# Adding to the residual by accumulating DMAs in the MLP stages of a hybrid decoder trunk

## The chip, the cores and the metric

The kernel runs on one core of one Trainium2 chip. The metric is device time in microseconds (us) of one execution. Three runs of the kernel before took 1236.65, 1238.46 and 1238.83 us; their median is 1238.46.

The core has five engines with a queue each, which run side by side and wait for each other by semaphores: TensorE (PE, the matmuls; PEld is its weight load), VectorE (DVE), ScalarE (ACT), GpSimd (POOL) and SyncE (SP, which here only starts transfers). Each engine works its own queue in order. Transfers (DMAs) are started from the queues of SP, ACT and POOL and are carried out by 16 DMA engines. Matmuls write to PSUM, from where DVE or ACT take the results; POOL works on the other on-chip memory, SBUF.

## What is computed

Two layers of a decoder trunk on x of 512 positions by 1024 features, in float32. Each layer first adds a mixing block (attention, short convolution and a recurrent part in parallel, then an output projection), then an MLP. What the change touches is the last two lines:

```python
for l in range(DEPTH):
    h = rms_norm(x, norm_mix_g[l])
    ...
    x = x + mixed @ w_out[l]
    h = rms_norm(x, norm_mlp_g[l])
    x = x + jnp.square(jax.nn.relu(h @ w_mlp_up[l])) @ w_mlp_down[l]
return rms_norm(x, final_norm_g)
```

The MLP is 1024 wide outside and 4096 inside.

## The kernel before

**Layout.** x is held transposed in SBUF, as eight tiles x[0] to x[7] of 128 features by 512 positions. A weight block is 128 by 128. To keep float32 accuracy, every weight and every operand is split into a rounded part and a remainder (`whi`/`wlo`, `mh`/`ml`, `shi`/`slo` and so on), and one product is three matmuls: hi x hi, hi x lo, lo x hi. The rounded part is made by ACT (a cast), the remainder by DVE or POOL (a subtraction). So each weight block costs a load, an ACT cast and a DVE subtraction before PE can use it.

**The mixing part** of each layer is ordered by hand. The MLP part, which the change touches, is written as a plain program, and the Tile framework orders each engine's queue from that program with its own estimate of times. Instructions of neighbouring groups are therefore interleaved. It also inserts every semaphore wait, and a buffer ring (`bufs=2` and so on) makes a new tile wait until the last user of its slot is done.

**The MLP of a layer.**
- `up(i)`, four plain up groups, and after that `two(i0, i1)`, fourteen paired up groups. `two` computes two up groups together from 2 x 2 blocks with seven half-width products in place of eight (Strassen's scheme in Winograd's form): sums of weight blocks (`s1` to `s4`) times sums of activation blocks (`th`, made once by `blocks`). Its products go to the PSUM tiles `pa`, `pb` and `pc`; ACT copies partial results out of PSUM (L1522, L1530, L1534, L1545), DVE adds them (L1541, L1546, L1549). The sums `s1` and `s3` of the next pair are made by DMA in `summed`: SP loads one weight half (L1475), then POOL's queue adds the other by an accumulating DMA (L1476).
- Each up result is squared and split by `square` and `kept` into `mh` and `ml` (POOL makes most `ml`, L1409). Four such tiles form the operand of one down step h.
- `down(h, js)` adds to x[j] what four middle tiles contribute. h runs from 0 to 7 (to 5 in the second layer, whose rest is `last_group`), and each h is done in two halves of four outputs j. A half is issued after each `two`, and the halves that are left come one behind the other at the end.
- A half of `down` is either **direct** or a **quad**. Direct (L1674 to L1679): for each j, twelve matmuls of 512 columns into one PSUM tile (`dn`), then one addition on DVE, `x[j] = pt + x[j]` (L1677). Quad (`quad`, for the pairs named in `DN_QUADS`: h = 2, 4, 6 in the first layer, h = 2, 4 in the second, both halves each): two pairs of outputs (j, j+1) with the same seven-product scheme at 256 columns. Its PSUM tiles are `qa`, `qb`, `qc`. `turn_blocks` prepares the activation sums for it.

**In a quad**, for each of its two j: r0 and r1 are raw weights (`rawq`, ring `raw` of three buffers, L1610), from which DVE makes the sums `s2q` and `s4q` (L1614 to L1618). ACT copies products out as `p1q`, `p5q`, `u2q`, `c1q` (L1599). DVE builds c0 in two halves: the left (L1634) and the right (L1644). c0 is the whole first output of the pair, 128 x 512, and is added to x[j] by DVE (`add`, L1595, seen in the trace as `x<-c0q`). The second output is added to x[j+1] in two halves of 256 columns (`x<-c1q` and `x<-qa`), also at L1595. c0 has a ring of two buffers (tag `c0`), which it shares with the c0 of `two` (L1541) and with `turn_blocks`. The ring with the tag `sq` has two buffers of 128 x 512 and serves the norms.

The loads of the raw weights all go through SP's queue, which waits in order for free buffers. POOL's queue holds in the MLP the `ml` remainders and the accumulating DMAs of `summed`.

Of the kernel before, what the change touches and what calls it, by code (L numbers as in the profile page):

```python
# [10 lines left out]
F32 = mybir.dt.float32  # L11
# [5 lines left out]
ALU = mybir.AluOpType  # L17
# [5 lines left out]
S = 512  # L23
P = 128
# [161 lines left out]
WHOLE = 5  # L186
PT = 1
N_TWO = (NG_UP - N_ONE) // 2
MID = tuple(range(N_ONE)) + tuple(N_ONE + i + N_TWO * j for i in range(N_TWO) for j in range(2))


# [82 lines left out]
def tile_trunk(ctx: ExitStack, tc: tile.TileContext, xT, wts, prm_d, cst_d, lora_d, gup_d, lam_d, fin_d, hd_d, out):  # L274
    nc = tc.nc
    act, dve, pool = nc.scalar, nc.vector, nc.gpsimd
# [23 lines left out]
    wp = Pool(ctx.enter_context(tc.tile_pool(name="wp", bufs=2)), "wp")  # L300
# [3 lines left out]
    def psum(tag, bufs, name):  # L304
        return ps.tile([P, 512], F32, tag=tag, bufs=bufs, name=name)
# [3 lines left out]
    x = [cp.tile([P, S], F32, tag=f"x{j}", name=f"x{j}") for j in range(NK)]  # L309
# [23 lines left out]
    def weights(g, k0=0, k1=NK, home=None):  # L333

        for a in range(k0, k1, 4):
            n = min(4, k1 - a)
            turn[0] += 1
            if home is None and spare[0] and turn[0] % (WB + 1) == 0:
                pool_, tags, bufs = spare[0], ("raw4", "whi4", "wlo4"), 1
            else:  # L340
                pool_, tags, bufs = wp, ("raw", "whi", "wlo"), WB
            raw = pool_.tile([P, 4, P], F32, tag=tags[0], bufs=bufs, name=f"raw{g}_{a}")
            nc.sync.dma_start(raw[:, :n].rearrange("p k c -> p (k c)"), wts[g, :, a * P:(a + n) * P])
            if home is None:
                hi, lo = [pool_.tile([P, 4, P], F32R, tag=t, bufs=bufs, name=f"w{p}{g}_{a}") for p, t in zip(("hi", "lo"), tags[1:])]
            else:
                hi, lo = home(a)
            act.copy(hi[:, :n], raw[:, :n])  # L348
            (pool if a and lean[0] else dve).tensor_tensor(lo[:, :n], raw[:, :n], hi[:, :n].bitcast(F32), ALU.subtract)  # L349
            for k in range(n):  # L350
                yield hi[:, k], lo[:, k]
# [9 lines left out]
    def mm3(out_ps, w, acts, n=NK):  # L361
        for _ in mm3_steps(out_ps, w, acts, n):
            pass
# [12 lines left out]
    def norm_tile(j, key):  # L376

        if j == 0:
            acc = wp.tile([P, S], F32, tag="acc", bufs=1, name=f"acc{key}")
            nrm[key] = [acc]  # L380
            act.activation(acc, x[j], AF.Square)
        else:
            sq = wp.tile([P, S], F32, tag="sq", bufs=2, name=f"sq{key}_{j}")
            act.activation(sq, x[j], AF.Square)
            dve.tensor_tensor(nrm[key][0], nrm[key][0], sq, ALU.add)
# [182 lines left out]
    for l in range(L):  # L568
# [826 lines left out]
        with ExitStack() as mx:  # L1395
# [73 lines left out]
            def summed(p, name):  # L1469

                if p < N_TWO:
                    i0, i1 = N_ONE + p, N_ONE + N_TWO + p
                    t = sums[p, name] = fp.tile([P, 4, P], F32, tag=name, bufs=2, name=f"{name}{l}_{i0}")
# [99 lines left out]
            def quad(h, half):  # L1573
# [9 lines left out]
                def product(pt, w, ks, moving, first, last):  # L1583
                    for i, k in enumerate(ks):
                        ahi, alo = moving(i)
                        whi, wlo = [t[:, k] for t in w]
                        pe.matmul(pt, whi, ahi, start=first and i == 0, stop=False, skip_group_check=True)
                        pe.matmul(pt, whi, alo, start=False, stop=False, skip_group_check=True)
                        pe.matmul(pt, wlo, ahi, start=False, stop=last and i == 1, skip_group_check=True)
# [4 lines left out]
                def add(j, q, pt):  # L1594
                    dve.tensor_tensor(x[j][:, q], pt, x[j][:, q], ALU.add)  # L1595

                def copied(name, pt, n):
                    t = fp.tile([P, H], F32, tag=name, bufs=2, name=f"{name}q{n}")
                    act.copy(t, pt)  # L1599
                    return t  # L1600
# [4 lines left out]
                for i in range(2):  # L1605
                    j = 4 * half + 2 * i
# [17 lines left out]
                for step in ((0, 1), (2, 3), (5, 4), (6,)):  # L1624
                    for j, w0, s12, s34, w22, (pa, pb, pc) in ab:
                        n = f"{l}_{h}_{j}"
                        for c in step:
                            if c == 0:
                                product(pa, w0, (0, 2), blk(0, 0), True, False)
                                keep["p1", j] = copied("p1", pa, n)  # L1630
                            elif c == 1:
                                product(pc, w0, (1, 3), blk(1, 0), True, True)
                                keep["c0", j] = c0 = fp.tile([P, S], F32, tag="c0", bufs=2, name=f"c0q{n}")
                                dve.tensor_tensor(c0[:, left], pc, keep["p1", j], ALU.add)  # L1634
                            elif c == 2:
                                product(pb, s12, (0, 1), trn(0), True, False)
                                keep["p5", j] = copied("p5", pb, n)
                            elif c == 3:
                                product(pa, s12, (2, 3), trn(1), False, False)
                                keep["u2", j] = copied("u2", pa, n)  # L1640
                            elif c == 5:
                                product(pb, s34, (2, 3), blk(1, 1), False, True)
                                c0 = keep["c0", j]
                                dve.tensor_tensor(c0[:, right], pb, keep["u2", j], ALU.add)  # L1644
                                add(j, slice(0, S), c0)
                            elif c == 4:
                                product(pa, s34, (0, 1), trn(2), False, False)
                                c1 = copied("c1", pa, n)
                                dve.tensor_tensor(c1, c1, keep["p5", j], ALU.add)
                                add(j + 1, right, c1)  # L1650
                            else:
                                product(pa, w22, (0, 1), trn(3), False, True)
                                add(j + 1, left, pa)

            def down(h, js):

                if (h, js[0] // 4) in DN_QUADS[l]:
                    quad(h, js[0] // 4)
                    return
                g, k0 = h // 2, 4 * (h % 2)  # L1660
                if h == 0 and js[0] == 0:
                    pts = [psum(("at", "mm")[j], 2, f"dn{l}_{h}_{j}") for j in js[:2]]
                    ws = [list(weights(wbase + NG_IN + NG_OUT + NG_UP + 8 * g + j, k0, k0 + 4)) for j in js[:2]]
                    for a, b in ((0, 3), (3, 4)):
                        for j, pt, w in zip(js, pts, ws):
                            for k in range(a, b):
                                (whi, wlo), (ahi, alo) = w[k], mids[k]
                                pe.matmul(pt, whi, ahi, start=(k == 0), stop=False)
                                pe.matmul(pt, whi, alo, start=False, stop=False)
                                pe.matmul(pt, wlo, ahi, start=False, stop=(k == 3))  # L1670
                    for j, pt in zip(js, pts):
                        dve.tensor_tensor(x[j], pt, x[j], ALU.add)
                    js = js[2:]
                for j in js:  # L1674
                    pt = psum(*(("mm", 2), ("rp", 4))[j % 2], f"dn{l}_{h}_{j}")
                    mm3(pt, weights(wbase + NG_IN + NG_OUT + NG_UP + 8 * g + j, k0, k0 + 4), mids[4 * h:4 * h + 4], 4)
                    dve.tensor_tensor(x[j], pt, x[j], ALU.add)  # L1677
                    if h == 2 * N_KG - 1 and j < NK - LATE:
                        norm_tile(j, f"m{l + 1}")  # L1679

# [8 lines left out]
            h, half = 0, 1  # L1689
            for p in range(N_TWO):  # L1690
                ms = two(N_ONE + p, N_ONE + N_TWO + p)
                if len(mids) >= 4 * h + 6 and h < 2 * N_KG - 2 * (l == L - 1):
                    down(h, range(4 * half, 4 * half + 4))
                    h, half = h + half, 1 - half
# [3 lines left out]
            while h < 2 * N_KG - 2 * (l == L - 1):  # L1698
                down(h, range(4 * half, 4 * half + 4))
                h, half = h + half, 1 - half  # L1700
# [11 lines left out]
def _layout(inputs):  # L1712
# [7 lines left out]
    for l in range(L):  # L1720
# [7 lines left out]
        for g in range(4):  # L1728
            w[b + 8 * g:b + 8 * g + 8] = groups(a["w_mlp_down"][l].reshape(NG_UP, P, D)[list(MID[8 * g:8 * g + 8])].reshape(D, D))
    prm = np.zeros((L, P, N_PRM), np.float32)  # L1730
# [41 lines left out]
```

## Time and profile before

| | |
|---|---|
| profiled execution | 1238.0 us, of which the span from first to last instruction is 1236.2 us |
| granted TensorE clock | 0.997 of full |
| accumulating DMAs from POOL's queue | 52, of 256 KB each |
| plain loads of weights from SP's queue | 323 (`raw`) and 40 (`rawq`) of 256 KB |
| DVE additions to x in the MLP | 68 direct (L1677), 20 `x<-c0q`, 20 `x<-c1q`, 20 `x<-qa` |
| matmuls | 10090 |

In the timeline views a row gives the start in us from the span's start, the length in us, the engine, the source line, the operation and its tiles (`out<-in`); a note in brackets gives the idle time of that engine just before the row and what ended it. Rows of one engine may overlap a little, since an instruction can start while the one before it still writes. A wait row gives who waited for whom, the us in total, how often, and the longest. PE's ends are modelled, so short idle times of PE read a little smaller than they are.

### The profile page before, as it was taken

The page shows a single profiled execution, that of the slowest core. Times are in us where ns is not written, and L with a number is a line of the kernel's source. Part 1 is how long each engine was busy: PE and PEld are TensorE (multiplying, and loading weights), DVE is VectorE, ACT ScalarE, POOL GpSimd, SP SyncE. Part 2 cuts the span into 40 slices and gives each one's busy share as a digit, 9 for nine tenths or more (in the row PEclk, how much of TensorE's full clock was granted, in tenths as well). Part 3 has the DMA queues.
Part 4 walks back from the last instruction along what each step waited for, and adds up shares of the span by engine and source line. Part 5 has one row for each costly group of instructions (what it writes and reads, how often), then busy time and mean ns, then how long its engine had stood idle before and what let it go on. Part 6 is the DMA issues. An engine that isn't in the chain of part 4 may idle for free. (4 is left out here: it accounts for less than half of the span.)

```text
span 1236.2 us, 26900 instructions
## 1 busy us (share of the span) xinstructions
PE 1217.8 (99%) x10090; PEld 1065.6 (86%) x10090; DVE 1011.3 (82%) x2023; ACT 742.6 (60%) x1606; POOL 386.0 (31%) x502
## 2 busy tenths in 40 slices
PE   9999999999999999999999999999999999999997
PEld 7788788888999989889888888888889898998987
DVE  7787888879888998989867777787897999899654
ACT  7785755557456655656675656564775566565543
POOL 2264636331122121121126354553302212222111
PEclk9999999999999999999999999999999999999998
DMA  6523333125653463631235243322456645446122
GB/s 225 159 90 108 111 86 102 53 96 169 190 146 108 128 180 98 168 86 52 94 113 159 82 133 118 94 70 69 145 172 147 152 110 158 128 118 177 54 78 77
DMA packets 95506, 148.48 MB, mean 120 GB/s; under 512 B 22544, under 2 KB 26384, under 8 KB 95376
## 3 DMA queue, kind: packets, MB, share of 16 engines
q1 hardware_dynamic: 87168, 132.39, 34.5%
q0 software_dynamic: 7488, 13.63, 7.2%
q8 instruction: 79, 1.29, 0.5%
q10 hardware_dynamic: 720, 0.75, 0.2%
q14 instruction: 51, 0.42, 0.1%
HBM read 137.56 MB, written 9.18 MB: 119 GB/s over the span
## 5 line engine op out<-in xcount | busy, mean ns | idle before, releaser
L694 POOL TENSOR_TENSOR wlo<-raw,whi 128x512 fp32r<-128x512 f32 x84 | 112.1, 1336 | 203.8 <-ACT whi L682 167.3
L287 PE MATMUL pj<-ahim,whi 128*128 128x512 f32 x392 | 156.7, 400 | 0.0
L287 PE MATMUL pj<-ahim,wlo 128*128 128x512 f32 x392 | 156.5, 399 | 0.0
L287 PE MATMUL pj<-alom,whi 128*128 128x512 f32 x392 | 156.0, 398 | 0.0
L1476 POOL DMA_DIRECT2D s<-wts x52 | 48.0, 922 | 293.3 <-DVE slo_p L1491 68.5
L1409 POOL TENSOR_TENSOR ml<-m,mh 128x512 fp32r<-128x512 f32 x56 | 82.3, 1518 | 178.9 <-ACT mh L1408 63.1
L682 ACT CAST whi<-raw 128x512 fp32r<-128x512 f32 x142 | 87.6, 618 | 70.3 <-PE pj L287 26.5
L287 PE MATMUL dn<-mh,whi 128*128 128x512 f32 x288 | 112.3, 390 | 0.0
L287 PE MATMUL dn<-ml,whi 128*128 128x512 f32 x288 | 112.2, 390 | 0.0
L287 PE MATMUL dn<-mh,wlo 128*128 128x512 f32 x288 | 112.1, 390 | 0.0
L1490 ACT CAST shi_p<-s 128x512 fp32r<-128x512 f32 x112 | 70.0, 625 | 65.1 <-PE pa L287 35.1
L287 PE MATMUL pa<-thi,shi_p 128*128 128x256 f32 x336 | 95.6, 285 | 4.5 <-ACT c L1545 3.9
L287 PE MATMUL pa<-tlo,shi_p 128*128 128x256 f32 x336 | 94.8, 282 | 0.0
L287 PE MATMUL pa<-thi,slo_p 128*128 128x256 f32 x336 | 94.4, 281 | 0.0
L1491 DVE TENSOR_TENSOR slo_p<-s,shi_p 128x512 fp32r<-128x512 f32 x112 | 76.5, 694 | 17.8 <-ACT shi_p L1490 16.6
L348 ACT CAST whi<-raw 128x512 fp32r<-128x512 f32 x86 | 52.9, 620 | 56.2 <-PE dn L287 30.7
L287 PEld LDWEIGHTS pj<-alom,whi 128*128 128x128 f32 x392 | 73.9, 188 | 14.0 <-issue 0.5
L287 PEld LDWEIGHTS pj<-ahim,wlo 128*128 128x128 f32 x392 | 73.9, 188 | 13.8 <-issue 0.2
L287 PEld LDWEIGHTS pj<-ahim,whi 128*128 128x128 f32 x392 | 73.8, 188 | 13.7 <-issue 0.3
L349 DVE TENSOR_TENSOR wlo<-raw,whi 128x512 fp32r<-128x512 f32 x86 | 72.5, 846 | 10.7 <-ACT whi L348 10.7
L1490 ACT CAST shi_p<-raw 128x512 fp32r<-128x512 f32 x84 | 52.4, 624 | 33.6 <-PE pb L287 18.1
L287 PEld LDWEIGHTS pa<-thi,shi_p 128*128 128x128 f32 x336 | 63.0, 188 | 6.1 <-ACT c L1545 4.7
(649 smaller groups left out, 3905.2 us busy)
## 6 DMA issues: line engine op xcount, KB each, us to landing
raw<-wts SPq DMA_DIRECT2D x323, 256.0 KB, 2.8
s<-wts SPq DMA_DIRECT2D x52, 256.0 KB, 3.6
s<-wts POOLq DMA_DIRECT2D x52, 256.0 KB, 4.4
rawq<-wts SPq DMA_DIRECT2D x40, 256.0 KB, 2.9
qs<-dqhi SPq DMA_DIRECT2D x24, 128.0 KB, 3.4
ks<-dkhi SPq DMA_DIRECT2D x24, 128.0 KB, 3.6
x<-xT SPq DMA_DIRECT2D x8, 256.0 KB, 4.8
dqhi<-qhi SPq DMA_DIRECT2D x6, 256.0 KB, 3.2
```

The lines of the kernel that those rows point to most:

```text
L287: ins = nc.tensor.matmul(*a, **k)
L348: act.copy(hi[:, :n], raw[:, :n])
L349: (pool if a and lean[0] else dve).tensor_tensor(lo[:, :n], raw[:, :n], hi[:, :n].bitcast(F32), ALU.subtract)
L682: yield act.copy(hi[:, k0:k1], raw[:, k0:k1])
L694: yield eng.tensor_tensor(lo[:, k0:k1], raw[:, k0:k1], hi[:, k0:k1].bitcast(F32), ALU.subtract)
L1409: (dve if i < 4 else pool).tensor_tensor(lo, m, hi.bitcast(F32), ALU.subtract)
L1476: pool.dma_start(t.rearrange("p k c -> p (k c)"), of[1], accum_op=ALU.add)
L1490: act.copy(hi, src)
L1491: dve.tensor_tensor(lo, src, hi.bitcast(F32), ALU.subtract)
```

## The change

It makes two edits, and adds a constant that names the direct down steps to which the second applies.

1. In a quad, the first output c0 is no longer added to x[j] by DVE, but by a DMA from POOL's queue that adds c0 to x[j] as it writes. There are 20 of these.
2. In the direct halves of h = 1, 3 and 5, the odd outputs (j = 1, 3, 5, 7) are no longer added by DVE from PSUM. ACT copies the PSUM tile to a tile `dx` of the ring `sq`, and a DMA from POOL's queue adds it to x[j]. There are 12 in each layer, 24 in all.

```diff
+BY_DMA = (1, 3, 5)
...
                                 c0 = keep["c0", j]
                                 dve.tensor_tensor(c0[:, right], pb, keep["u2", j], ALU.add)
-                                add(j, slice(0, S), c0)
+                                pool.dma_start(x[j], c0, accum_op=ALU.add)
...
                     mm3(pt, weights(wbase + NG_IN + NG_OUT + NG_UP + 8 * g + j, k0, k0 + 4), mids[4 * h:4 * h + 4], 4)
-                    dve.tensor_tensor(x[j], pt, x[j], ALU.add)
+                    if j % 2 and h in BY_DMA:
+                        t = wp.tile([P, S], F32, tag="sq", bufs=2, name=f"dx{l}_{h}_{j}")
+                        act.copy(t, pt)
+                        pool.dma_start(x[j], t, accum_op=ALU.add)
+                    else:
+                        dve.tensor_tensor(x[j], pt, x[j], ALU.add)
```

## The prediction

> **What bounds the kernel now.** I read the page first, then a table of busy time by stretch, then who waited for whom, then the time lines round the waits.
>
> ```profile
> span 1236.2 us, 26900 instructions
> PE 1217.8 (99%) x10090; PEld 1065.6 (86%) x10090; DVE 1011.3 (82%) x2023; ACT 742.6 (60%) x1606; POOL 386.0 (31%) x502
> ```
>
> TensorE (PE) is busy 99% of the span, and the change takes no matmul away. So all that can be won is idle time of PE: 1236.2 - 1217.8 = 18.4 us, and only the part of it that lies in the MLP stages, where the edited lines run. The stretches that hold the second quad of a pair, beside the one that follows the first pair (columns: busy time of PE, PEld, DVE, ACT, POOL with instruction counts, clock, DMA share, GB/s):
>
> ```profile
> 394.00:437.00 43.00, 41.42 (x342) 40.69 (x341) 40.95 (x81) 27.72 (x63) 9.18 (x8) 1.00 0.48 139
> 437.00:478.00 41.00, 41.00 (x260) 37.21 (x259) 35.48 (x66) 22.13 (x43) 9.74 (x9) 1.00 0.53 138
> 478.00:522.00 44.00, 41.92 (x346) 41.14 (x345) 42.17 (x83) 28.55 (x64) 9.68 (x8) 1.00 0.51 140
> 1001.00:1044.00 43.00, 41.29 (x341) 40.56 (x340) 40.81 (x81) 27.71 (x63) 9.70 (x8) 1.00 0.49 139
> 1086.00:1129.00 43.00, 41.05 (x339) 40.32 (x338) 40.55 (x80) 27.70 (x62) 9.61 (x8) 1.00 0.52 134
> ```
>
> Four stretches, one for each pair of quads that stands among the paired up groups, lose 1.58, 2.08, 1.71 and 1.95 us of PE. In them VectorE (DVE) is busy 94 to 96%. In the direct down groups between them (second row) PE loses nothing and DVE is at 87%. The clock is 1.00 throughout. What PE waits for there, from the waits of its weight load (us in total, times, longest), whose times are not modelled:
>
> ```profile
> PEld pa L287 <- ACT c L1545: 4.7, 4, 1.4
> PEld qa L287 <- ACT p1q L1599: 3.7, 4, 1.1
> ...
> PEld qa L287 <- ACT c1q L1599: 1.4, 4, 0.4
> ```
>
> Four times each: 4.7 after a pair, 3.7 + 1.4 = 5.1 inside the second quad. Together 9.8 us, the ceiling of what I count on.
>
> **First part: the quad's 20 first sums leave DVE.** The wait of 4.7, at its first occurrence (DVE, then ACT, then PE):
>
> ```profile
> 425.85 0.68 DVE L1595 TENSOR_TENSOR x<-c0q,x 128x512 f32<-128x512 f32 x1
> 426.45 0.42 DVE L1649 TENSOR_TENSOR c1q<-c1q,p5q 128x256 f32<-128x256 f32 x1
> ...
> 427.45 0.69 DVE L1595 TENSOR_TENSOR x<-c0q,x 128x512 f32<-128x512 f32 x1
> ...
> 433.59 0.69 DVE L1499 TENSOR_TENSOR s<-s,raw 128x512 f32<-128x512 f32 x1
> 434.20 0.42 DVE L1541 TENSOR_TENSOR c<-pc,p 128x256 f32<-128x256 f32 x1
> ```
>
> ```profile
> 431.55 0.62 ACT L1490 CAST shi_p<-s 128x512 fp32r<-128x512 f32 x1 [0.53 <-ACT u L1534]
> 434.39 0.62 ACT L1490 CAST shi_p<-s 128x512 fp32r<-128x512 f32 x1 [2.22 <-PE pb L287]
> 434.92 0.37 ACT L1545 COPY c<-pa 128x256 f32<-128x256 f32 x1
> ```
>
> ```profile
> 435.34 0.39 PE L287 MATMUL pa<-thi,shi_p 128*128 128x256 f32 x1 [0.91 <-ACT c L1545]
> ```
>
> PE stands for the copy at L1545, the copy stands behind a cast on in-order ACT, and the cast stands for `s`, which DVE makes at 433.59. No row of DVE from 425.85 to 434.20 bears an idle note: it has work queued without a break, and the two `x<-c0q` are in that queue. One of them holds DVE for 426.45 - 425.85 = 0.60 us (its 0.68 overlaps the next), so taking both out brings `s` 1.2 us forward, to 432.4. The cast before it on ACT ends at 432.2, so it does not hold it. The copy follows 1.2 us earlier and PE's wait, 4.7 / 4 = 1.17 on average, goes: 4 x 1.17 = **4.7 us**. What is late next is DVE's own queue after 434.2, which moves forward by the same 1.2 and meets a down group, where DVE has slack.
>
> The wait of 5.1 has another root, a load:
>
> ```profile
> 402.73 0.68 DVE L1595 TENSOR_TENSOR x<-c0q,x 128x512 f32<-128x512 f32 x1
> ...
> 408.67 0.68 DVE L1491 TENSOR_TENSOR slo_p<-raw,shi_p 128x512 fp32r<-128x512 f32 x1
> ...
> 409.94 0.42 DVE L1618 TENSOR_TENSOR s4q<-rawq,s2q 128x256 f32<-128x256 f32 x1
> ...
> 410.88 0.42 DVE L1541 TENSOR_TENSOR c<-pc,p 128x256 f32<-128x256 f32 x1
> ...
> 414.88 0.43 DVE L1614 TENSOR_TENSOR s2q<-rawq 128x256 f32<-128x256 f32 x1 [2.05 <-DMA rawq<-wts]
> ```
>
> ```profile
> 407.44 0.62 ACT L1490 CAST shi_p<-raw 128x512 fp32r<-128x512 f32 x1 [0.55 <-PE pb L287]
> ...
> 416.06 0.62 ACT L1579 CAST shi_6b<-s2q 128x512 fp32r<-128x512 f32 x1 [3.83 <-DVE s2q L1615]
> ```
>
> DVE frees the weight buffer at 409.94, the last raw weights of the second quad land at 414.9, ACT has stood for 3.83 us, and the copy p1q that PE wants comes behind the casts that piled up. Here 1.2 us of DVE time is not 1.2 us of lead: `slo_p<-raw` at 408.67 needs the cast that ends at 407.44 + 0.62 = 408.06, so at most 0.6 comes forward. The upper bound is 4 x 0.6 = 2.4 us.
>
> **Below, this term is bounded by the added DMA traffic.** The nearest rows are today's accumulating DMAs of the weight sums, the same 256 KB on the same queue (q0: packets, MB, share of the 16 engines):
>
> ```profile
> q0 software_dynamic: 7488, 13.63, 7.2%
> ```
>
> ```profile
> L1476 POOL DMA_DIRECT2D s<-wts x52: 856/886/1237, 286.8 to 1137.1; - x52
> ```
>
> ```profile
> DMA to landing us min/median/max: 3.8/4.4/6.9
> ```
>
> 0.072 x 1236.2 / 52 = 1.71 us of all 16 engines for each. Should two of them stand ahead of the decisive load in full, it lands 3.4 us later, and 3.4 - 0.6 = 2.8 us are lost four times: -11.2. But the first sum of the earlier quad is ready by 402.73 and the second some 1.6 us later (425.85 and 427.45 show the spacing), so with 4.4 to land both are through near 409, before the load is issued near 409.4. The value lies near the upper end; for loads they push back a little I take under half of it, **1.0 us**. The Trainium skill (DMA: Bandwidth & Descriptors, "Anatomy of one DMA — SWDGE (gpsimd) path") fits a POOL DMA as 2.0 us plus bytes over 436e3 per us, which by my estimate is 2.6 us for 256 KB; the trace disagrees with 4.4, and by the page the bound of -11.2 would shrink to some 4 x (2 x 0.6 - 0.6) = -2.4. The measured 1.71 and 4.4 decide.
>
> **Buffers.** The DMA holds c0 (two buffers) until it lands. The next user of the first one is `c<-pc` at 410.88, about 1.2 earlier after the change: 409.7 - 402.7 = 7.0 us, against 0.9 of issue at most in front and 4.4 (longest 6.9) to land. Cost nothing at the median; what it costs beyond is a rival. The next addition to the same x comes with the direct down group in the stretch from 437 on, so its wait for the landing is free.
>
> **POOL.** 44 issues of 0.89 are 39 us more on an engine with 9 of 43 us busy in these stretches. Behind them stand the weight sums and the `ml` remainders; they are pushed back by one or two issues, under 2 us, and I find no idle note of PE or ACT that names either in these stretches. Taken at nothing; if that cover were gone, 2 us for each of four pairs, 8 us.
>
> **Second part: 24 odd outputs of direct groups go through ACT.**
>
> ```profile
> L1677 DVE TENSOR_TENSOR x<-dn,x x68: 675/684/700, 308.8 to 1160.9; 128x512 f32<-128x512 f32 x68
> ```
>
> ```profile
>   PE dn L287: 21.2, 19
> ```
>
> ```profile
> L1351 ACT COPY pT<-ptt 128x512 f32<-128x512 f32 x12 | 7.0, 587 | 7.6 <-PE ptt L292 7.4
> ```
>
> DVE loses 24 x 0.60 = 14.4 us, ACT gains 24 x 0.59 = 14.1 us (the nearest row is a PSUM copy of the same shape), in stretches where ACT is busy 22 of 41 us and PE never waits. Nothing on the path, so **0**. DVE stood 21.2 us in 19 turns at the head of its queue for a dn product; ACT inherits some of that, 1.1 us each, with weight casts behind it. These are used a group of twelve matmuls later, so I price it at nothing; if the cover fails, 24 x 1.1 = 26 us.
>
> **Sum.** 4.7 + 1.0 = 5.7 us. The profiled execution took 1238.0 (span 1236.2 and 1.8 round it): 1238.0 - 5.7 = **1232.3**. The median of the runs is 1238.46, so the profiled one is fair; a difference under 0.2%, 2.5 us, cannot be told from none.
>
> **Rivals.**
> *The stall moves.* The order of the MLP stages is planned from estimated times, so it is planned anew; DVE at 95% and ACT late by 3.83 us in the second quad leave little room, and a wait of the same kind can come back at another copy. For it: both engines are full there. Against: 1.2 us of DVE work per quad is really gone. Half of the 4.7 comes back and the 1.0 is lost: 1238.0 - 2.3 = 1235.7, to no gain at 1238. Chance 0.20.
> *The load lands later (slower).* Place: the second quad's raw weights. Each us that the accumulating DMAs add is lost four times; break-even with the 4.7 is a delay of 0.6 + 1.17 = 1.8 us, half of the 3.4 of two such DMAs. At the full 3.4 the time is 1238.0 - 4.7 + 11.2 = 1244.5. For it: DVE stands 2.05 us for that load now, and the DMA share rises from 0.5 by 4 x 1.71 / 43 = 0.16. Against: both should be through by 409. Chance 0.13.
> *c0 is held (slower).* From 7.0 us between the sum and its landing on, DVE stands at L1541 with all its queue behind it. At 9.0, 2.0 us for each of the 8 quads that a paired group follows, 16 us, less the 5.7: 1248. The issue would have to stretch. The Trainium skill (SBUF — State Buffer, "SBUF: two separate sides") warns of just that: while DVE runs in a two-port mode GpSimd "cannot write the descriptors", and in "A bandwidth-pool intuition that's wrong" it gives some 3.1 us for a 0.62 us DMA. No run here shows that: 52 issues take 0.86 to 1.24 us beside a DVE at 82%. Chance 0.05.
> That the additions do not become DMAs is excluded by the 52 that run this way.
>
> **How the numbers follow.** Forecast 0.62, the stall that moves 0.20, the late load 0.13, c0 held 0.05. The forecast's own range is 1238.0 - 9.8 = 1228.2 to 1235.7. To hold 0.8 the whole reaches from 1228 to 1239, which takes in most of the first rival and leaves out the tails of the slower ones. Faster by over 0.2% (under 1236.0) are the forecast and a little of the first rival, less a forecast that falls short: 0.62; within 0.2% 0.21; slower (over 1240.9) 0.17.
>
> **What would show it.** Right: the four stretches keep PE at 1.00 or nearly, `pa <- ACT c L1545` falls from 4.7 to under 1, `qa <- ACT p1q` stays at 2.5 to 3.7, x<-c0q is gone from DVE, x<-dn is down to 44, POOL's DMAs are up to 96 at about 0.9 us, DVE is near 983 us busy. Wrong: DVE's wait for rawq grows beyond 2 us each, or DVE or ACT waits name a landing of x, c0 or dx, or POOL's issues exceed 2 us, or a new wait of PE names another producer.

## The result and the profile after

The changed kernel takes **1243.39 us** (median of 5 runs, 1241.8 to 1246.99); the kernel before took 1238.46 us in the same comparison. The ratio is 1.0048, 95% interval 1.003 to 1.0066: slower by about 6 us (4.9 by the medians), where 1232.3 us were forecast. Below, a difference between kernels is worked out from ratios to the kernel before, times 1238.4 us; a ratio's half width of some 0.001 makes each good to 1 to 2 us.

The page of the changed kernel (lines of the file moved by one or two; `p1q` is copied at L1600, `p` at L1523, the new DMAs stand at L1646 and L1681):

```profile
span 1241.4 us, 27076 instructions
PE 1220.0 (98%) x10090; PEld 1068.4 (86%) x10090; DVE 987.5 (80%) x1979; ACT 754.1 (61%) x1630; POOL 425.2 (34%) x546
...
q0 software_dynamic: 13824, 25.17, 12.5%
```

DVE went from 1011.3 to 987.5 us as meant, and PE stands idle for 1241.4 - 1220.0 = 21.4 us in place of 18.4. The four stretches round the second quads, with the same columns as before:

```profile
397.00:440.00 43.00, 42.46 (x339) 41.35 (x338) 40.65 (x81) 29.62 (x65) 13.25 (x13) 1.00 0.72 180
483.00:527.00 44.00, 40.99 (x311) 40.10 (x310) 38.39 (x76) 26.52 (x60) 13.05 (x12) 0.92 0.68 170
1004.00:1047.00 43.00, 40.39 (x336) 39.94 (x335) 38.83 (x78) 28.38 (x63) 13.04 (x12) 1.00 0.57 147
1089.00:1132.00 43.00, 40.32 (x336) 39.87 (x335) 38.76 (x78) 28.34 (x63) 12.41 (x11) 1.00 0.62 152
```

They lose 0.54, 3.01, 2.61 and 2.68 us of PE, and the second has a clock of 0.92 where it had 1.00. The waits of the weight loads say for what:

```profile
PEld qa L288 <- ACT p1q L1600: 9.7, 4, 3.2
PEld pa L288 <- ACT p L1523: 2.7, 5, 1.3
```

The wait for `c` of 4.7 us is gone from this list. In its place the wait for `p1q` rose from 3.7 to 9.7 us, and the wait for `p` from 1.1 to 2.7 us. DVE's wait for the rawq load rose too; the rows of the kernel before, and then the new one:

```profile
PEld pa L287 <- ACT p L1522: 1.1, 3, 0.8
...
DVE s2q L1614 <- DMA rawq<-wts: 9.5, 6, 2.4
```

```profile
DVE s2q L1615 <- DMA rawq<-wts: 11.7, 6, 3.2
```

**Why p1q is late.** ACT round the same second quad, in the kernel before:

```profile
500.43 0.62 ACT L1579 CAST shi_6b<-s2q 128x512 fp32r<-128x512 f32 x1 [3.84 <-DVE s2q L1615]
501.19 0.63 ACT L1418 ACTIVATE m<-m 128x512 f32<-128x512 f32 x1
501.73 0.35 ACT L1599 COPY p1q<-qa 128x256 f32<-128x256 f32 x1
```

and in the changed one:

```profile
501.06 0.62 ACT L1580 CAST shi_6b<-s2q 128x512 fp32r<-128x512 f32 x1 [4.16 <-DVE s2q L1616]
502.08 0.62 ACT L1580 CAST shi_6c<-s4q 128x512 fp32r<-128x512 f32 x1 [0.40 <-DVE s4q L1619]
502.61 0.61 ACT L1491 CAST shi_p<-raw 128x512 fp32r<-128x512 f32 x1
503.13 1.14 ACT L1419 ACTIVATE m<-m 128x512 f32<-128x512 f32 x2
504.18 1.12 ACT L1409 CAST mh<-m 128x512 fp32r<-128x512 f32 x2
505.20 0.40 ACT L1580 CAST whi_6d<-rawq 128x256 fp32r<-128x256 f32 x1
505.51 0.63 ACT L1600 COPY p1q<-qa 128x256 f32<-128x256 f32 x2
```

Both times ACT stands about 4 us for `s2q`, that is, for the rawq load that DVE waits for. Before, one instruction lay between the cast it stood for and the first p1q copy, and the copy ran 1.3 us after the cast had begun. Now seven lie between, and it runs 4.45 us after. The planner laid out ACT's queue anew: in all four second quads of the changed kernel that lie among paired up groups the copy comes behind `whi_6d`.

**What the wait does to the clock.** PE at that place, and the 6 us after it:

```profile
502.52 0.28 PE L288 MATMUL qb<-dlo,shi_4b 128*128 128x256 f32 x1
502.63 0.28 PE L288 MATMUL qb<-dhi,slo_4b 128*128 128x256 f32 x1
505.93 0.58 PE L288 MATMUL qa<-dhi,shi_4b 128*128 128x256 f32 x1 [3.01 <-ACT p1q L1600]
506.30 0.41 PE L288 MATMUL qa<-dlo,shi_4b 128*128 128x256 f32 x1
506.52 0.41 PE L288 MATMUL qa<-dhi,slo_4b 128*128 128x256 f32 x1
```

```profile
506.00:512.00 6.00, 6.00 (x29) 6.00 (x30) 5.21 (x9) 3.09 (x8) 2.20 (x2) 0.52 0.51 162
```

Matmuls of 256 columns, 0.12 us apart before the wait, follow at 0.21 us after it: the granted clock is 0.52 for 6 us. At 0.12 us each, the 29 matmuls of this row would take 3.5 us: by this estimate some 2.5 us are lost beside the wait itself.

### The profile page after: what moved, and what is told of

It reads as the page before. It is cut to its first block, busy times and chain, and to the rows that moved or that the text cites. A ratio compares the mean times of both kernels' runs of the same rounds, so it can differ in the third digit from the quotient of the medians.

```text
span 1241.4 us, 27076 instructions
## 1 busy us (share of the span) xinstructions
PE 1220.0 (98%) x10090; PEld 1068.4 (86%) x10090; DVE 987.5 (80%) x1979; ACT 754.1 (61%) x1630; POOL 425.2 (34%) x546
## 4 chain that ended last, share of the span: by engine, by line
PE 87%; DVE 6%; ACT 3%; DMA 2%; issue 2%; POOLq 0%; POOL 0%; ACTq 0%; DVEq 0%
PE pj L288 22%; PE dn L288 14%; PE pa L288 12%; PE po L288 8%; PE pb L288 6%; PE qa L288 4%; PE dnF L288 4%; PE pc L288 3%; PE up L288 2%; PE qb L288 2%; PE sc L288 1%; DMA raw<-wts 1%; PE ptt L293 1%; PE pg L288 1%; DMA rawq<-wts 1%
```

## Experiments

Three theories stood against each other after this. **Order**: the late p1q copy in ACT's queue costs the time. **Traffic**: the added DMAs slow the weight loads. **Part two**: the odd outputs are what costs.

**1. The quads' part alone.** `BY_DMA = ()`: all odd outputs go through DVE.

> Only the 20 first sums of the quads go by DMA; the 24 odd outputs stay on VectorE. Order theory (with the first sums off VectorE the planner puts ScalarE's copy p1q of the second quad behind eight other ScalarE instructions, which stand behind the raw weights' load): the wait for c at the paired groups, 4.7 us, is gone, the wait for p1q is 9 to 10 us in place of 5.1, with a drop of the granted clock where one of them passes 3 us; 1239 to 1243 us. Traffic theory (the added DMAs delay that load): the same 1239 to 1243 us, with each wait of VectorE for rawq longer by about as much as PE's wait. Part-two theory (the odd outputs are what costs): 1233 to 1235 us.

1238.03 us, ratio 0.9994 (0.9985 to 1.0003): no change, where the prediction had 5.7 us for this part. None of the three ranges was met: the time lies under those of order and traffic and over that of part two, and p1q, for which order had 9 to 10 us, shows 6.6:

```profile
PEld qa L288 <- ACT p1q L1600: 6.6, 4, 2.2
```

The wait for c is gone, the late copy is there, and p1q went from 3.7 to 6.6 us. So p1q takes back 2.9 of the 4.7 us. PE's busy time rose by 1.8 us as well, from 1217.8 to 1219.6; behind the longest p1q wait, 2.2 us, the clock fell for 3.4 us (last section), which was forecast only for waits over 3 us.

**2. The odd outputs alone.** The 20 first sums go back to DVE (`add(j, slice(0, S), c0)`).

> Only the 24 odd outputs of direct groups go through ScalarE and a DMA; the quads stay on VectorE. Order theory: p1q keeps its place of before, so the waits for c and p1q stay at 4.7 and 5.1 us, and what is seen is the second part's own cost, the longer waits for the copy p at the start of paired groups and at the first direct group of the second layer, some 2 us: 1238.5 to 1241 us. Part-two theory: 1242 to 1244 us. Traffic theory: 24 DMAs, none of them just ahead of the rawq load, 1238 to 1240 us.

1243.03 us, ratio 1.0032 (1.002 to 1.0044): 4.0 us slower. This is in the range of part two alone. The part that was priced at nothing is the dear one. ACT's order in the second quads is that of before, so this is not the late copy.

**3. The quads' part without its DMAs.** The 20 first sums are left out entirely, so x lacks them; odd outputs through DVE; the copy is late as in experiment 1.

> The quads' first sums are not added to x at all, neither by VectorE nor by DMA (this part of the computation is left out), and the odd outputs stay on VectorE. ScalarE's planned order has p1q behind the same eight instructions as in the changed kernel, but there is no added DMA. Order theory: PE waits for p1q 8 to 10 us in four turns as with the DMAs, 1238 to 1243 us. Traffic theory: the wait for p1q is back at 5 us or less and the one for c is gone, 1232 to 1234 us.

1234.7 us, ratio 0.9969 (0.9957 to 0.998). Order missed by over 3 us, and its 8 to 10 us for p1q came out as 6.2; traffic came nearer, with a time 0.7 us over its range, but p1q did not fall to 5. Behind the late copy the 20 transfers cost 0.9994 - 0.9969 = 0.0025, 3.1 us. Little of that is the p1q wait (6.6 and 6.2 us); in the two profiled executions it is PE's busy time (1219.6 and 1216.3 us), of which the fall of the clock in experiment 1 is a part. The rest stays open.

**4. Only the second quads by DMA.** `if half: pool.dma_start(...) else: add(...)`, odd outputs through DVE.

> Only the second quad of each pair adds its first sums by DMA (10 DMAs); the first quad of each pair adds on VectorE as before, and so do the odd outputs. ScalarE's planned order up to p1q is that of before. Order theory: the wait for c (4.7 us) goes, the wait for p1q stays at about 5 us: 1233 to 1235 us, faster than both kernels. Traffic theory: these DMAs come after the decisive load, so 1233 to 1235 us as well. Part-two theory: 1238 us or less. If the wait for c comes back in another place, 1237 to 1239 us.

1234.14 us, ratio 0.9962 (0.995 to 0.9975): 4.7 us faster than before, with ten of the 20 additions moved, as both order and traffic had it. The wait for c is gone, and ACT keeps the order of before:

```profile
500.26 0.62 ACT L1580 CAST shi_6b<-s2q 128x512 fp32r<-128x512 f32 x1 [3.24 <-DVE s2q L1616]
...
501.34 0.35 ACT L1600 COPY p1q<-qa 128x256 f32<-128x256 f32 x1
```

So the c wait goes with the second quad's additions alone, and the queue turns over only when the *first* quad's leave DVE too. The first quad's alone were not tried.

**5. The late copy in the kernel before, nothing else.**

```diff
-                                keep["p1", j] = copied("p1", pa, n)
+                                with tc.issue_after(last) if half and h < 6 and j == 4 else ExitStack():
+                                    keep["p1", j] = copied("p1", pa, n)
```

> Nothing of the change is in this kernel: all additions stay with VectorE. In the four second quads ahead of the last one, ScalarE's copy of the first p1q is put behind the cast whi_6d, where the changed kernel has it. Theory 'order' (the copy stands behind casts that wait for VectorE and so for the rawq load): the p1q wait of TensorE's weight loads grows from 3.7 us to 5.5 to 10 us, and the time by 1.5 to 5 us, to 1240 to 1243 us. Rival 'traffic' (the transfers make the loads late, the order does nothing): 1238.5 us, with p1q near 4 us.

1240.15 us, ratio 1.0017 (1.0008 to 1.0025): 2.1 us slower, at the low end of what order forecast. The profiled execution, 1238.15 us, is the fastest of the twelve:

```profile
PEld qa L287 <- ACT p1q L1601: 7.9, 4, 2.3
...
PEld pa L287 <- ACT c L1545: 1.9, 4, 1.1
```

p1q grew by 4.2 us, and c shrank by 2.8. The mean granted clock of the twelve runs is 0.998 in two of them (1238.15 and 1239.18 us), 0.992 in the slowest (1244.2 us) and 0.995 to 0.997 between; the 23 runs of the kernel before beside them have 0.997 or 0.998. The longest p1q wait of the profiled run, 2.3 us, left the clock whole. That the longer runs are those in which such a wait cost the clock fits their lower means, but only the profiled run has a trace.

**6. The quads' part with the copy put back.** As experiment 1, with the first product and its p1q copy of a second quad issued ahead of the casts for the next pair.

```diff
+                    if half and h < 6 and i:
+                        product(pa0, w00, (0, 2), blk(0, 0), True, False)
+                        keep["p1", j0] = copied("p1", pa0, f"{l}_{h}_{j0}")
+                        first.append(made[-1])
...
+                    with tc.issue_after(first[0]) if first else ExitStack():
+                        act.copy(hi, src)
```

> All 20 first sums by DMA, odd outputs with VectorE as before, and the first p1q copy put back ahead of the casts of the second pair. Theory 'order': the p1q wait falls from 6.6 us (quad sums by DMA with the late copy) to 4 us or less, the c wait stays gone, and the time is 1233 to 1236 us. Rival 'traffic' (the loads are late because of the 20 transfers): the p1q wait stays at 5 to 7 us, and the time at 1237 to 1239 us.

**1232.83 us**, ratio 0.9957 (0.9944 to 0.997): 5.3 us faster than the kernel before. ACT, and then the waits of the weight loads:

```profile
497.44 0.62 ACT L1581 CAST shi_6b<-s2q 128x512 fp32r<-128x512 f32 x1 [2.91 <-DVE s2q L1621]
498.99 0.63 ACT L1419 ACTIVATE m<-m 128x512 f32<-128x512 f32 x1 [0.93 <-DVE m L1418]
499.52 0.36 ACT L1603 COPY p1q<-qa 128x256 f32<-128x256 f32 x1
```

```profile
PEld qa L288 <- ACT p1q L1603: 3.4, 5, 1.2
```

Same additions, same 20 transfers as experiment 1, and in the traces the order of ACT, DVE and SP differs from it only in the four second quads and the few us behind them: 0.9994 - 0.9957 = 0.0037, 4.6 us, are the place of four copies in ACT's queue and what moves with it. Order is shown; traffic alone does not explain experiment 1.

**7. Twenty transfers more on the kernel before.** `pool.dma_start(x[j], rs, accum_op=ALU.add)` behind each DVE addition; x holds 20 terms too many.

> The kernel before, order of ScalarE and VectorE unchanged, with 20 accumulating DMAs more: each adds the tile rs to x at the place where a first sum is added, so x holds 20 additions that the reference does not have. It puts the traffic of the quads' part on the kernel and nothing else. Theory 'traffic': the waits for the rawq and raw loads grow, and the time rises by 2 to 4 us, to 1240.5 to 1242.5 us. Theory 'order': within 1 us of the kernel before, 1237.5 to 1239.5 us.

1244.52 us, ratio 1.0044 (1.0032 to 1.0056): 5.4 us slower, more than traffic forecast and against order as the only cause. So there are two causes.

```profile
PEld qa L287 <- ACT p1q L1599: 8.5, 8, 1.7
...
DVE s2q L1614 <- DMA rawq<-wts: 14.9, 6, 4.2
```

The p1q copy is in its old place and still late, because the rawq load lands later: DVE's wait for it rose from 9.5 to 14.9 us. These transfers begin about 3 us later than those of experiment 6 (tile x; ns shortest, median and longest, first and last start). First this kernel, then that of experiment 6:

```profile
L1646 POOL DMA_DIRECT2D x<-rsf x20: 874/1200/1577, 405.5 to 1127.6; - x20
```

```profile
L1658 POOL DMA_DIRECT2D x<-c0q x20: 874/898/1249, 402.8 to 1116.2; - x20
```

The first quad's two transfers land at 411.0 and 413.3 us here, at 406.1 and 410.8 in experiment 6. The decisive rawq load is not slower in itself (4.2 us from issue to landing, 4.4 before); the loads ahead of it land later, and it is issued at 411.3 in place of 410.4. That the shift by 3 us makes the whole difference is argued, not tried: DVE also keeps its additions here.

**8 to 10. What of the odd outputs costs.** All three have, on PE, DVE, ACT and SP, the same instructions in the same order as experiment 2, and differ in what POOL does after ACT's copy. In 8 the DMA is left out, in 9 two memsets of the copied tile stand in its place, in 10 it moves 64 of the 512 columns; x lacks these terms, or seven eighths of them.

```diff
-                        pool.dma_start(x[j], t, accum_op=ALU.add)
```

> First sums with VectorE as before; the 24 odd outputs are copied out by ScalarE, and the DMA that would add each to x is left out, so x lacks these 24 terms. Theory 'plan' (VectorE's and ScalarE's work is laid out in another order when the additions leave VectorE, the split of a weight tile meets GpSimd's ml, and the copy stands ahead of p): the time stays near the 1243.0 us of the run with the DMAs, 1241.5 to 1243.5 us. Rival 'DMA' (the transfers and GpSimd's standing at their issue, 34.9 us in all, make ml and the loads late): it falls to 1237 to 1239.5 us.

```diff
-                        pool.dma_start(x[j], t, accum_op=ALU.add)
+                        pool.memset(t, 0.0)
+                        pool.memset(t[:, 0:S // 2], 0.0)
```

> As the run with the odd outputs copied and no DMA (1237.59 us), with GpSimd's part put back without its transfer: in the place of each of the 24 DMAs GpSimd waits for ScalarE's copy and then fills the copied tile with two memsets, about as long as an issue took (0.88 us). x lacks these 24 terms. Theory 'stand' (GpSimd stands at the issue, 34.9 us in all, and its ml behind it comes late): 1241.5 to 1243.5 us. Rival 'transfer' (the 256 KB that each DMA moves delay the loads): 1237 to 1238.5 us.

```diff
-                        pool.dma_start(x[j], t, accum_op=ALU.add)
+                        pool.dma_start(x[j][:, 0:64], t[:, 0:64], accum_op=ALU.add)
```

> As the run with the odd outputs alone by DMA (1243.03 us), same order on all engines, but each of the 24 DMAs adds only 64 of the tile's 512 columns: an eighth of the bytes, the same 128 partitions and the same issue and wait. x lacks seven eighths of these 24 terms. Theory 'transfer', by bytes: 1237.5 to 1239 us. Theory 'stand': 1242 to 1243.5 us. Between them if the cost goes by descriptors.

| POOL after the copy | us | ratio to before |
|---|---|---|
| 8: nothing | 1237.59 | 0.9993 (0.9984 to 1.0002) |
| 9: stands, no transfer | 1239.62 | 1.0006 (0.9996 to 1.0016) |
| 10: an eighth of the bytes | 1239.87 | 1.0009 (0.9999 to 1.002) |
| 2: the whole DMA | 1243.03 | 1.0032 (1.002 to 1.0044) |

The theory "plan", that the additions' leaving DVE lays out DVE and ACT worse, falls with experiment 8: same layout, and the 4.0 us are gone. Between 8 and 2 lie 0.0039, 4.8 us. Most of it, 0.0023 or 2.8 us, comes with the other seven eighths of the bytes. Queue q0 carries 10944 packets in both 10 and 2, so this part goes by bytes and not by packets. The rest, 2 us, comes with what 10 keeps, POOL's standing, the issue and the packets, but the intervals of 8, 9 and 10 overlap. 9 met neither theory's range; 10 lies between its two, where its expectation put a cost by descriptors. The waits of 10 and then of 2 show where the bytes act:

```profile
PEld pa L288 <- ACT p L1523: 3.5, 5, 1.8
PEld qa L288 <- ACT p1q L1600: 2.1, 3, 1.0
...
DVE s2q L1615 <- DMA rawq<-wts: 8.1, 6, 1.9
```

```profile
PEld qa L288 <- ACT p1q L1600: 4.0, 6, 1.2
PEld pa L288 <- ACT p L1523: 3.4, 5, 1.3
...
DVE s2q L1615 <- DMA rawq<-wts: 10.5, 8, 3.0
```

The rawq wait rises by 2.4 us and p1q by 1.9, while p stays. It is the same load as in experiment 7, and the same copy behind it. Against experiment 8, which has no transfers, the rawq wait rises from 7.6 to 10.5 us, p1q from 1.6 to 4.0 and p from 2.2 to 3.4: 3.6 of the 4.8 us stand in PE's two waits. Against the kernel before (9.5 and 3.7 us) the rise is small, since in experiment 8 both are lower than there.

**11. The whole change with the copy put back.** Experiment 6 with `BY_DMA = (1, 3, 5)`.

> The whole change, with the first p1q copy put back ahead of the casts of the second pair: the quads' kernel of 1232.83 us with the odd outputs by DMA as well. If order and transfers add: 1232.83 + 5.4 = 1238 us, 1237 to 1239.5 us, and no p1q wait over 3 us and no drop of the clock. If the late copy had no part in the changed kernel's time: 1242 to 1243.5 us.

1237.29 us, ratio 0.9991 (0.9981 to 1.0002), clock 0.997 or 0.998 in all runs.

```profile
PEld qa L288 <- ACT p1q L1603: 4.5, 4, 1.2
```

The odd part costs 0.9991 - 0.9957 = 0.0034, 4.2 us, on top of experiment 6, as it did alone. The changed kernel is 1.0048 - 0.9991 = 0.0057, 7 us, slower than this one, and the two differ in no more than the place of the copies and the order the planner draws from it, again only round the second quads. The p1q wait grows by 5.2 us between them, and the rest is of the size of the clock's drop (0.992 to 0.995 in the five runs of the changed kernel).

**12. Experiment 6 without its DMAs.** The line `pool.dma_start(x[j], c0, accum_op=ALU.add)` is taken out, so x lacks 20 first sums.

> The kernel of 1232.83 us (all first sums by DMA, early p1q copy), the 20 DMAs left out and nothing in their place: x lacks the 20 first sums. It gives the price of the 20 transfers where the order is right. Theory 'transfer' with a price as under the late order (1238.03 against 1234.7, 3.3 us): 1228.5 to 1230.5 us. If transfers only cost where the copy is late: 1232 to 1233.5 us.

1234.19 us, ratio 0.9961 (0.9948 to 0.9975): no faster than with the transfers (0.9957), and 0.7 us over the range that had it so. Where the copy is in its place, the 20 transfers cost nothing that can be measured. Four kernels now differ in two things, and their ratios to the kernel before are:

| | with the 20 transfers | without them |
|---|---|---|
| copy late | 0.9994 (experiment 1) | 0.9969 (experiment 3) |
| copy in its place | 0.9957 (experiment 6) | 0.9961 (experiment 12) |

The late copy costs 4.6 us with the transfers and 0.0008, 1.0 us, without them, which the intervals do not tell from none. The transfers cost 3.1 us behind the late copy and nothing behind the early one. So neither theory holds by itself in the quads' part: it is the two together that cost.

**The account**, in us against before: quads' part with the copy in its place -5.3, odd outputs +4.2, copy late +7.0, in all +5.9; measured 1.0048, +5.9. The sum closes by its making, since each step is one kernel further, and the price of the late copy holds for this order of the steps: it was 1.0 us without transfers, 4.6 with 20, 7.0 with 44. What is shown is that each step exists, and that the odd part costs the same with and without the quads' part (4.2 and 4.0).

## Why the prediction was wrong

Two steps failed: the first part's working held ACT's order fixed, and the second part's DMAs were priced at nothing.

**The ceiling and the c wait: right.** PE's idle time in those stretches was the only thing to win. The c wait went entirely once the second quad's additions had left DVE (experiments 1, 4 and 6), and experiment 4 gained the 4.7 us of the sum. The note on the cast at 434.39 names PE's pb and not DVE's `s`; that the wait went bears out the reading through `s`.

**The p1q term: wrong by its cause.** The prediction gave it +1.0 us, bounded by how far the load can move, and took ACT's queue as it stood. But it also said that the MLP is "planned anew", and priced that as a rival of 0.20, from half of the 4.7 given back (1235.7 us) to no gain at 1238. Experiment 1, at 1238.03 us, is the far end of that rival. The step that failed is the argument "at most 0.6 comes forward": it followed dependences with ACT's order held fixed. The order changed, the copy moved behind seven instructions, and by the waits the term became -2.9 us in experiment 1 and -6.0 in the changed kernel (9.7 against 3.7). With the copy in its place, in experiment 6, the term is +0.3, and the kernel takes 1232.83 us where the sum said 1232.3: the working of the first part holds for the kernel that it assumed.

**The late load: a rival with the right mechanism and the wrong place.** Its price went by the quad's own transfers. These cost nothing by themselves (experiment 12), but not for the reason given: they were not through near 409. In the changed kernel the second starts 2.6 us after the first and not 1.6, takes 5.7 us and lands at 411.9, after the rawq load was issued at 410.6; and the load that was put near 409.4 in the kernel before stands at 410.42 in SP's rows, 409.38 being another. It landed early all the same (413.4 us, 414.8 before). That part of the forecast was luck. The 24 transfers of the second part reach the same rawq load (10.5 us of wait in experiment 2, 8.1 in experiment 10), and the prediction had no line for their traffic.

**The second part at 0: the other failed step.** It counted 14.4 us that leave DVE and 14.1 that enter ACT, and found both covered. That was right (experiment 8: 0.9993). It left out that the additions come back as 24 x 256 KB through the DMA engines, each 1.71 us of all sixteen by the prediction's own figure, and with POOL standing for ACT's copy:

```profile
POOL x L1681 <- ACT dx L1680: 36.2, 16, 4.3
```

A working that prices a DMA in one part of a change has to price it in the other. The 26 us "if the cover fails" was a price for ACT's standing, which did not come about.

**Buffers: right.** The new DMAs in the changed kernel:

```profile
L1681 POOL DMA_DIRECT2D x<-dx x24: 864/880/1145, 361.5 to 1167.2; - x24
L1646 POOL DMA_DIRECT2D x<-c0q x20: 869/894/1214, 403.6 to 1125.3; - x20
```

```profile
x<-dx POOLq DMA_DIRECT2D x24, 256.0 KB, 4.0
x<-c0q POOLq DMA_DIRECT2D x20, 256.0 KB, 4.2
```

An issue takes 0.88 to 0.89 us and a landing 4.0 to 4.2 us, near the 0.89 and 4.4 taken; the fit that the prediction drew from the Trainium skill (DMA: Bandwidth & Descriptors, "Anatomy of one DMA — SWDGE (gpsimd) path") gave 2.6 us and does not agree. The longest landing of an `x<-c0q` was 8.2 us, beyond the 7.0 from which DVE was to stand, but no wait names a landing of x or c0. The stretched issue of which the Trainium skill (SBUF — State Buffer, "SBUF: two separate sides") warns did not appear: the longest took 1.21 us. What POOL's standing costs, taken at nothing, is not settled: experiment 9 lies 1.6 us over experiment 8, and their intervals overlap.

**The signs.** The c wait, the 44 `x<-dn` left on DVE, POOL's 96 DMAs and DVE's busy time came as listed. PE at 1.00 in the four stretches did not: one of the four comes near. And p1q, to stay at 2.5 to 3.7 us, showed 9.7, with DVE's rawq wait at 1.95 us in the mean of its six turns. ACT's rows in their order show the queue, which the sum of the waits does not.

## What to carry to other kernels

Where a planner orders the queues from estimated times, an edit to one engine's work can reorder another's. A forecast that moves instructions along the old rows is a forecast for the old order; pin the order of the copies that PE waits for (here four, worth 4.6 us with the quads' part, 7 with the whole change and 1, not told from none, without transfers), and then judge the edit. An addition turned into a DMA is not free where the engine it leaves was no bound: price its bytes against the load that lands last, and ask at what moment they start, since the same 20 transfers cost nothing in experiment 6 while twenty that start 3 us later cost 5.4 us in experiment 7 (that the start is the reason was not tried by itself). The version to keep is that of experiment 6: the quads' first sums by DMA, p1q early, odd outputs on DVE. Experiment 4, with the second quads' sums alone by DMA, is not told from it (0.9962 and 0.9957) and needs no order by hand.

## What the runs showed of the hardware

The granted clock falls to one half in the last 10 us of each of the fourteen profiled executions. Ahead of that it fell in two of them: in the changed kernel, behind a p1q wait of 3.2 us, from 504.91 to 511.74 us, and in experiment 1, behind one of 2.2 us, from 504.76 to 508.18 us. Waits of 2.8 and 2.9 us in the changed kernel and of 2.3 us in experiment 5 left it whole. So the length of the wait does not decide by itself.

The two falls lasted 6.83 and 3.41 us, and the fall at the end begins 212 and 211 times 3.41 us after them; in every trace the changes stand on such a grid. Cut into stretches on it, PE's busy time (right behind the length) and the clock (third from the right) read as follows. Experiment 1:

```profile
501.35:504.76 3.41, 1.41 (x13) 1.20 (x11) 3.41 (x7) 3.41 (x9) 1.06 (x1) 1.00 0.23 77
504.76:508.18 3.42, 3.42 (x16) 3.42 (x17) 3.42 (x6) 2.22 (x6) 2.22 (x2) 0.50 0.52 155
```

The changed kernel, ahead of its fall and at the wait of 2.8 us:

```profile
501.50:504.91 3.41, 1.41 (x12) 1.21 (x11) 3.41 (x8) 3.01 (x7) 0.00 (x0) 1.00 0.25 77
1027.15:1030.57 3.42, 2.33 (x20) 2.12 (x18) 3.42 (x9) 2.95 (x6) 0.00 (x0) 1.00 0.67 148
1030.57:1033.98 3.41, 1.89 (x15) 1.89 (x16) 3.41 (x7) 3.41 (x10) 2.90 (x2) 1.00 0.21 79
```

Experiment 5:

```profile
501.05:504.47 3.42, 1.82 (x16) 1.61 (x14) 3.39 (x7) 3.39 (x7) 1.59 (x2) 1.00 0.02 6
504.47:507.88 3.41, 2.96 (x24) 2.96 (x25) 3.41 (x6) 3.40 (x11) 1.71 (x2) 1.00 0.28 88
```

Both falls follow a stretch in which PE stood for 2.00 us. The longer wait of 2.8 us was split by a boundary into 1.09 and 1.52 us, and experiment 5 has 1.60 us in one stretch: no fall. The falls at the end of the fourteen traces follow stretches with 1.58 to 2.26 us, and no stretch that left the clock whole has more than 1.64. What decides, by these traces, is how much idle time of PE falls into one stretch of the grid; the edge lies near 1.6 us, as far as PE's modelled ends tell. No run was made to test it.

A stretch at half clock lowers the mean clock by 3.41 x 0.5 / 1238 = 0.0014. Against the 0.9975 or so of the kernel before, the mean of 0.995 in the changed kernel's profiled run is by this estimate its two stretches, and 0.992 some four; each can cost up to 1.7 us. With this it fits that the late copy alone spread the runs from 1238.15 to 1244.2 us. The Trainium skill (TensorE: Matmul & The Clock Gate, "Why this matters for your kernels") asks for no idle gap of PE over some 3 us between bursts of matmuls, or the clock falls back to half. The wait of 3.2 us agrees; experiment 1 does not, where a gap of 2.2 us was enough, and the measurement decides.
